# A hybrid RG-LRU, Conformer, cross-attention and conv-FFN layer: query weights and memory tokens turned as float32r, and the stages' order set anew

## Chip, cores and metric

The kernel runs on one core of a Trainium2 chip. The metric is device time in microseconds, the median of three runs. A core has a matrix engine (TensorE, PE in the profile; its loads of the stationary operand are PEld), a vector engine (VectorE, DVE), a scalar engine (ScalarE, ACT), GpSimd (POOL) and SyncE (SP), which here mostly issues DMAs. SBUF is the on-chip memory, PSUM the banks that TensorE writes.

## What is computed

One layer over x of 2048 tokens by 1024 channels and 256 memory tokens, all float32:

```python
h = rms_norm(x, mix_norm_g);  z = h @ w_in                    # 1024 -> 2048
lru_x, lru_gate, conf_a, conf_b = split(z, 4)                 # 512 each
y_lru = rg_lru(causal_dwconv(lru_x, 4 taps)) * gelu(lru_gate) # 8 heads of 64, scan over tokens
c = causal_dwconv(conf_a * sigmoid(conf_b), 31 taps)
c = silu(layer_norm(c))
x = x + concat([y_lru, c]) @ w_out

h = rms_norm(x, xa_norm_g);  m = rms_norm(mem, mem_norm_g)
q = h @ w_q;  k, v = split(m @ w_kv, 2)                       # 4 heads of 256
p = softmax(q @ k.T / 16)                                     # over 256 memory tokens
x = x + (p @ v) @ w_o

h = rms_norm(x, ffn_norm_g);  g, u = split(h @ w_up, 2)       # 3072 each
x = x + (gelu(causal_dwconv(g, 3 taps)) * u) @ w_down
out = rms_norm(x, final_norm_g)
```

## The kernel before

**Arithmetic.** Most matmuls run three times in float32r: each operand is split into a rounded part (ACT copies it into a float32r tile, names ending in h) and the rest (DVE subtracts, names ending in l), and hh, hl and lh are added up in PSUM (`mm3`). `split` and `split_scaled` do the splitting. A float32r tile has to be written by an instruction that writes that type; a float32 tile can't simply be read as one.

**Turning.** TensorE contracts over partitions, so tokens and weights are turned where their layout does not fit: `transpose` multiplies a 128 x 128 block by the identity (`ident`), as float32, four blocks into one PSUM bank. Turned are x (tiles `x`, `xn`), the softmax's output (`prob`), some gains, the memory tokens (`mem`, 16 blocks, in `memory_a`) and the query weights (`raw`, 64 blocks, in `operands` inside `memory_a`).

**Stages.** The tokens are worked in four blocks q of 512. For each block a mixer (`m[q]`: norm, projection by `w_in`, conv, LRU), a normalisation (`n[q]`) and attention (`a[q]`). Attention is folded: `memory_a` forms A = w_q k^T for each head (it needs the turned query weights and `kv`, the projection of the memory tokens by `w_kv`), and `memory_vo` forms v w_o; both are kept in DRAM. Blocks 2 and 3 are attended together (`attend_pair`) by a Strassen-like scheme of seven products, whose weights the task `fold` prepares. Then comes the feed-forward: `up` over two halves of 1024 tokens (`strassen_cols`, seven products for each pair of weight columns, operand sets B11, B21, T2, T1, T3, T4, B22, tiles `Xh` and `Xl`), and `Down` (tiles `hidh`, `hidl`, `wh`, `wl`).

`HalfX.make(key)` splits the four blocks of one operand set, each by an ACT copy and a DVE subtraction. `first_x` makes the first `EARLY` sets of the first half ahead of time; `up` makes the others when a product asks for them. For the second half, `up` makes each set in the last step of the first half, as soon as the set that it replaces has been used.

**Order.** The order of instructions is written out when the kernel is built, in two steps. First the stages are Python generators (`Task`); `drive` lets the first one in the list `TURNS` go on whose pause is over, counted in TensorE time. What a task yields is a pause or another task that it waits for; the constants (`MEM_WAIT`, `MIX_WAIT`, `ATT_PACE` and so on) are such pauses. Second, `Program` plans all operations on a model of the engines: it takes costs from `estimate`, a handover between engines of `HOP`, DMAs of `DMA_DELAY` plus bytes by `DMA_RATE`, ACT table switches (`ACT_SWITCH`, and `ACT_PATIENCE`, how near its due time an operation must be before a switch is made for it), gives each operation a due time, and picks on each engine the ready one that is due first. Operations made while `pr.first` is set come before all others. The best of `PASSES` plans is emitted. On the chip each engine then works through its list in that order and waits where an operand is late. DMAs are issued in the plan's order by SP, a few by ACT and POOL. Tiles come from 84 SBUF slots of 128 x 512 (`S`), a few larger ones, and 8 PSUM banks.

**The beginning.** `make_identity` builds `ident` on POOL, DVE sets a few constants, and `first_tokens` keeps TensorE busy with 16 turns of the identity while the first x and `w_in` pieces and the mixing gains (`in_mix_norm_g`, issued by ACT) arrive.

Nearly every instruction comes from `Program.emit`, so line 399 stands in almost every row of the profile, and rows are told apart by the tiles.

Of the kernel before, what the change touches and what calls it, by code (L numbers as in the profile page):

```python
# [12 lines left out]
F32R = mybir.dt.float32r  # L13
AF = mybir.ActivationFunctionType
# [3 lines left out]
P = 128  # L18
# [3 lines left out]
KQ = NK // 2  # L22
TT = 512
NQ = S // TT
# [3 lines left out]
M = 256  # L28
# [19 lines left out]
            AF.Gelu_apprx_tanh: (11,), AF.Silu: (18,)}  # L48


HOP = 0.3
HOP_SAME = 0.1
DMA_DELAY = 2.5
DMA_RATE = 300e3
ACT_SWITCH = 1.3
ACT_PATIENCE = 8.0
POOL_LAST = 6.0
ISSUE = dict(SP=0.1, ACT=0.3, Pool=1.0)
PASSES = 3
# [32 lines left out]
class Ref:  # L92
# [2 lines left out]

    def __getitem__(self, i):
        return Ref(self.buf, self.steps + (lambda ap: ap[i],), self.dummy[i])

    def f32(self):
        return Ref(self.buf, self.steps + (lambda ap: ap.bitcast(F32),), self.dummy)  # L100
# [32 lines left out]
class Program:  # L133
# [71 lines left out]
    def dma(self, out, in_, reads=(), writes=(), join=False, slack=30, by="SP"):  # L205
# [5 lines left out]
        nbytes = max(int(np.prod(r.dummy.shape)) for r in refs) * 4  # L211
        o.cost, o.delay = nbytes / DMA_RATE, DMA_DELAY
        o.calls.append(("dma_start", (), dict(out=out, in_=in_)))
# [25 lines left out]
    def deadlines(self, order):  # L239
# [10 lines left out]
        for o in reversed(self.ops):  # L250
            lat = o.cost + o.delay + HOP
            for s in o.succs:
# [7 lines left out]
    def schedule(self):  # L260
# [27 lines left out]
        def pick(e, t):  # L288
# [22 lines left out]
            if e == "ACT":  # L311
                o = h[0][2]
                if o.sets is not None and table[0] not in o.sets and o.due + lag[0] - t > ACT_PATIENCE:
                    other = [x for x in h if x[2].sets is None or table[0] in x[2].sets]
# [43 lines left out]
        while events:  # L358
# [11 lines left out]
            else:  # L370
                for s in o.succs:
                    satisfied(s, t + (HOP_SAME if s.eng == o.on else HOP))
                for b in o.bufs:
                    b.left -= 1
                    if b.left == 0:
                        free[b.tag].append(b.slot)
                        grant(b.tag, t + HOP)
        assert len(order) == len(self.ops)
# [44 lines left out]
def hybrid_layer(  # L423
# [7 lines left out]
    nc = tc.nc  # L431
# [9 lines left out]
    pr = Program(nc, place)  # L441

    def const(shape, name, dtype=F32):
        return Buf(None, shape, cpool.tile(list(shape), dtype, name=name), dtype, name)
# [10 lines left out]
    def transpose(o, in_, idn):  # L455
        pr.do("PE", "transpose", o, in_, idn)

    class together:
        def __enter__(self):
            pr.group = pr.op("PE")  # L460
# [10 lines left out]
    def rnd(name, shape=None):  # L471
        return pr.new("S", shape, F32R, name)
# [7 lines left out]
    def spawn(gen, before=None):  # L480
        t = Task(gen)
        tasks.insert(tasks.index(before) if before else len(tasks), t)
        return t
# [15 lines left out]
    ident_t = cpool.tile([P, P], F32, name="ident")  # L499
    make_identity(nc, ident_t)  # L500
    ident = Buf(None, (P, P), ident_t)
    ones_t = cpool.tile([P, P], F32, name="ones")
    nc.vector.memset(ones_t[:], 1.0 / DL)
    ones = Buf(None, (P, P), ones_t)
# [124 lines left out]
    def raw_cols(w, c0, kq):  # L629
        st = pr.new("W", (P, KQ, 2 * P), name="raw")  # L630
        pr.dma(st[:], w[kq * KQ * P : (kq + 1) * KQ * P, c0 : c0 + 2 * P].rearrange("(k p) f -> p k f", p=P))
        return st
# [119 lines left out]
    def turned(xs, take, wait=0):  # L752
        for k in range(NK):
            p = ps()
            with together():
                for tb in range(NTB):
                    transpose(p[:, tb * P : (tb + 1) * P], xs[tb][k // 4][:, (k % 4) * P : (k % 4 + 1) * P], ident[:])
            take(k, p)
            if k % 2:
                yield wait  # L760
# [191 lines left out]
    def memory_a():  # L952
        pr.first = True
        xs = []
        for mb in range(2):
            parts = []
            ssp = small(2)
            for half in range(2):
                t = tmp("mem")
                pr.dma(t[:], mem[0, mb * P : (mb + 1) * P, half * TT : (half + 1) * TT])  # L960
                ACT(junk[:], t[:], AF.Square, accum_out=ssp[:, half : half + 1])
                parts.append(t)
            r = small(1)
            V("tensor_tensor", r[:], ssp[:, 0:1], ssp[:, 1:2], op=ALU.add)
            ACT(r[:], r[:], AF.Sqrt, bias=eps[:], scale=1.0 / D)
            V("reciprocal", r[:], r[:])
            for t in parts:
                ACT(t[:], t[:], AF.Copy, scale=r[:, 0:1])
            xs.append(parts)
        for k2 in range(NK // 2):  # L970
            t = tmp("mt")
            p = ps()
            with together():
                for kk in range(2):
                    k = 2 * k2 + kk
                    for mb in range(2):
                        transpose(p[:, kk * M + mb * P : kk * M + (mb + 1) * P], xs[mb][k // 4][:, (k % 4) * P : (k % 4 + 1) * P], ident[:])
            for kk in range(2):
                sl = slice(kk * M, (kk + 1) * M)
                ACT(t[:, sl], p[:, sl], AF.Copy, scale=vec["v1024"][:, 2 * k2 + kk, G_MEM : G_MEM + 1])  # L980
            mt.append(t)
        pr.first = False
        yield MEM_WAIT
        def operands(h):
            kk = yield from kv(h * M)
            yield 0

            qt = []
            for kq in range(2):
                st = raw_cols(w_q[0], h * M, kq)  # L990
                for db in range(2):
                    p = ps()
                    with together():
                        for j in range(KQ):
                            transpose(p[:, j * P : (j + 1) * P], st[:, j, db * P : (db + 1) * P], ident[:])
                    hi, lo = pair("qt")
                    split(p[:], hi, lo)
                    qt.append((hi, lo))
            yield 1
            return kk, qt  # L1000

        nxt = yield from operands(0)
        for h in range(4):
            (kh, kl), qt = nxt
            if h < 3:
                nxt = yield from operands(h + 1)
            for k2 in range(NK // 2):
                p = ps()
                with together():
                    for kk in range(2):  # L1010
                        k = 2 * k2 + kk
                        for db in range(2):
                            hi, lo = qt[(k // KQ) * 2 + db]
                            cs = slice((k % KQ) * P, (k % KQ + 1) * P)
                            ks = slice(db * M, (db + 1) * M)
                            mm3(p[:, kk * M : (kk + 1) * M], hi[:, cs], lo[:, cs], kh[:, ks], kl[:, ks], db == 0, db == 1)
                t = pair("a")
                split(p[:], *t)
                for kk in range(2):
                    keep(A_rows, 2 * k2 + kk, h // 2, slice((h % 2) * M, (h % 2 + 1) * M), [b[:, kk * M : (kk + 1) * M] for b in t])  # L1020
                yield 0
            yield 0
# [56 lines left out]
    attended = [Task(None) for _ in range(NQ)]  # L1079
# [893 lines left out]
        yield V_LATE  # L1973
        vec["v3072"] = columns([ffn_conv_w[0], ffn_conv_b], DFF, "v3072")

    EARLY, VO_WAIT, V_LATE, Z_COPIED = 5, 2, 500, (0, 1)
    MIX_WAIT, MIX_TURN, LN_SUM, LN_SQ, GATES = (5, 7, 6, 0), 5, 6, 0, 3
    MIX_PACE, ATT_PACE = (1, 4, 3, 4), ((0, 3, 0), (0, 2, 2), (6, 3, 3), (5, 9, 0))
    PAUSE, WARM = 2, 16
    FED = ("B21", "T2", "T1", "T3")  # L1980
    MEM_WAIT, VO_LATE, ATT_TURN, FFN_TURN, X_PACE, T_PACE = 17, 10, 1, (3, 8, 7, 24), 3, 10

    FOLDED = (2, 3)
    PAIR_WAIT, PAIR_TURN, FOLD_PACE = (0, 0, 9, 17), 7, (6, 7, 35)
    EARLY_AT, KEPT_AT = 6, 5
    FOLD_AT = lambda: ([turned_x[0]], [mem_a, turned_x[1]], [mem_vo])
    F_out, F_a, F_vo = Folds(W_out, "t_out"), Folds(A_rows, "t_a"), Folds(VO_rows, "t_vo")

    NORMED = [lambda: ([m[0]], 108), lambda: ([attended[0]], 31), lambda: ([m[2]], 26), lambda: ([m[3], n[2]], 6)]
    ATTEND = [lambda: [n[0]], lambda: [n[1]]]  # L1990
    TURNS = lambda: [later, first, fold, m[0], mem_a, m[1], first_t, a[0], n[2], m[3], n[0], n[3], mem_vo, n[1], m[2], a[1], a[2], tail]
    X = [HalfX(h) for h in range(NH)]

    def first_x():
# [6 lines left out]
    def feed_forward():  # L2001
        yield first
        yield attended[NQ - 1]
        spawn(X[1].kept(attends[NQ - 1], 20), tail)
        spawn(prepare_down(), tail)
        yield from up(0, X[0], X[1].make)
        down = Down()

        def ahead(key):
            if key in FED:  # L2010
                down.feed(0, FED.index(key))

        yield from up(1, X[1], ahead)
        yield from down.run()

    mixers, normeds, attends = ([Task(None) for _ in range(NQ)] for _ in range(3))
    later, mem_a, mem_vo, first_t, first, tail = (Task(None) for _ in range(6))
    m, n, a = mixers, normeds, attends
# [7 lines left out]
    fold = Task(fold_weights())  # L2026
# [36 lines left out]
```

## Time and profile before

| What | Value |
|---|---|
| median of three runs | 2398.5 us (2398.17 to 2398.66) |
| span of the profiled execution | 2396.1 us, 2.4 us under the median |
| instructions | 33,483 |
| PE busy | 2382.6 us, 99% of the span, 10,948 matmuls |
| PEld busy (beside PE) | 1974.5 us, 82% |
| DVE busy | 2034.0 us, 85% |
| ACT busy | 1313.2 us, 55%, in it 75 table loads of 1.28 us |
| granted TensorE clock | 0.999 of full speed |
| DMA | 604.56 MB, mean 252 GB/s |

A row of a group reads: line, engine, operation, tiles written and read, shapes, number, then busy time, mean ns of one, and the idle time ahead of it with what ended it. A matmul's row names the moving operand first and then the stationary one: `ps<-ident,raw` is a turn of a piece of `raw`. Matmul records overlap, each lasts longer than the distance to the next, so a matmul's cost is read from the distance between starts. A row of the waits has the time in all, the number of times, and the longest. A row of stretches has the stretch, its length, busy time and count of each engine, the granted clock, the busy share of the DMA engines, and GB/s.

### The profile page before, as it was taken

How to read it: one execution, taken by the hardware profiler on the slowest of the kernel's cores; microseconds unless marked ns; L12 is line 12 of the kernel's file. 1: busy time of each engine (PE TensorE's matmuls, PEld its weight loads, DVE VectorE, ACT ScalarE, POOL GpSimd, SP SyncE). 2: the span in 40 equal slices, each digit the busy share in tenths (PEclk: the TensorE clock that was granted, in tenths of full speed). 3: DMA queues.
4: the chain of work that ended last, by engine and by line, in shares of the span. 5: the costliest groups of instructions: out<-in, count | busy, mean ns of one | idle time of the engine just before them, and what ended most of it. 6: DMA issues, size and time to landing. Idle time of an engine off the chain costs nothing.

```text
span 2396.1 us, 33483 instructions
## 1 busy us (share of the span) xinstructions
PE 2382.6 (99%) x10948; PEld 1974.5 (82%) x10948; DVE 2034.0 (85%) x3355; ACT 1313.2 (55%) x2374; POOL 11.2 (0%) x26
## 2 busy tenths in 40 slices
PE   9999999999999999999999999999999999999998
PEld 7898888888887888888888888888888888888887
DVE  7999994299899869879999887988988896676787
ACT  7772776357557678695555555554555541222333
POOL 1000000000000000000000000000000000000000
PEclk9999999999999999999999999999999999999999
DMA  9598789775878988787766544556565589887986
GB/s 351 197 296 309 234 300 305 254 255 176 296 261 271 318 277 280 268 289 265 252 234 208 194 172 158 175 177 211 190 216 199 186 303 324 283 280 254 312 303 258
DMA packets 363912, 604.56 MB, mean 252 GB/s; under 512 B 34809, under 2 KB 116985, under 8 KB 363738
## 3 DMA queue, kind: packets, MB, share of 16 engines
q1 hardware_dynamic: 362952, 601.81, 73.8%
q8 instruction: 86, 1.41, 0.2%
q14 instruction: 88, 0.72, 0.1%
q0 software_dynamic: 640, 0.36, 0.0%
q10 hardware_dynamic: 146, 0.27, 0.0%
HBM read 409.36 MB, written 192.94 MB: 251 GB/s over the span
## 4 chain that ended last, share of the span: by engine, by line
PE 94%; DVE 2%; ACT 2%; DMA 1%; issue 1%; SPq 0%; POOL 0%; DVEq 0%; POOLq 0%; ACTq 0%
PE ps L399 94%; DMA wl<-w_down 1%; DVE conv L399 1%; ACT L399 0%; DMA raw<-in_w_kv_dram 0%; ACT wh L399 0%; DVE wl L399 0%; ACT gate L399 0%; DVE x L399 0%; DVE s L399 0%; ACT yh L399 0%; DVE smalls L399 0%; DVE ptl L399 0%; ACT prob L399 0%; ACT conv L399 0%
## 5 line engine op out<-in xcount | busy, mean ns | idle before, releaser
L399 PE MATMUL ps<-Xh,wh 128*128 128x512 f32 x1344 | 523.3, 389 | 0.7 <-ACT u L399 0.7
L399 PE MATMUL ps<-Xh,wl 128*128 128x512 f32 x1344 | 523.2, 389 | 0.7 <-DVE wl L399 0.5
L399 PE MATMUL ps<-Xl,wh 128*128 128x512 f32 x1344 | 523.0, 389 | 0.0
L399 PE MATMUL ps<-wh,hidh 128*128 128x512 f32 x960 | 374.4, 390 | 0.0
L399 PE MATMUL ps<-wh,hidl 128*128 128x512 f32 x960 | 374.2, 390 | 0.1
L399 PE MATMUL ps<-wl,hidh 128*128 128x512 f32 x960 | 373.7, 389 | 0.0
L399 DVE SCALAR_TENSOR_TENSOR conv<-cb,v,conv 128x512 f32<-128x512 f32 x480 | 334.9, 741 | 1.8 <-ACT conv L399 0.9
L399 PEld LDWEIGHTS ps<-Xh,wl 128*128 128x128 f32 x1344 | 252.3, 188 | 54.0 <-DVE wl L399 1.5
L399 PEld LDWEIGHTS ps<-Xh,wh 128*128 128x128 f32 x1344 | 252.3, 188 | 53.1 <-ACT u L399 1.1
L399 PEld LDWEIGHTS ps<-Xl,wh 128*128 128x128 f32 x1344 | 252.3, 188 | 52.5
L399 ACT ACTIVATE hidh<-s 128x512 fp32r<-128x512 f32 x186 | 113.8, 631 | 271.6 <-DVE s L399 227.9
L399 PEld LDWEIGHTS ps<-wh,hidl 128*128 128x128 f32 x960 | 180.2, 188 | 39.5 <-DVE hidl L399 2.1
L399 PEld LDWEIGHTS ps<-wh,hidh 128*128 128x128 f32 x960 | 180.2, 188 | 37.8 <-ACT hidh L399 0.4
L399 PEld LDWEIGHTS ps<-wl,hidh 128*128 128x128 f32 x960 | 180.3, 188 | 37.2 <-DMA wl<-w_down 0.4
L399 PE MATMUL ps<-xh,wh 128*128 128x512 f32 x512 | 204.0, 398 | 0.1
L399 PE MATMUL ps<-xl,wh 128*128 128x512 f32 x512 | 199.6, 390 | 0.3 <-DVE xl L399 0.3
L399 PE MATMUL ps<-xh,wl 128*128 128x512 f32 x512 | 199.6, 390 | 0.0
L399 ACT ACTIVATE wh<-s 128x512 fp32r<-128x512 f32 x192 | 119.6, 629 | 117.6 <-DVE s L399 79.1
L399 ACT ACTIVATE wh<-raw 128x512 fp32r<-128x512 f32 (+2 forms) x214 | 127.4, 613 | 53.1 <-PE ps L399 21.6
L399 ACT ACTIVATE u<-ps 128x512 f32<-128x512 f32 x144 | 85.7, 595 | 126.0 <-PE ps L399 125.2
L399 DVE TENSOR_TENSOR acc<-acc,ps 128x512 f32<-128x512 f32 (+1 forms) x157 | 102.7, 678 | 59.5 <-PE ps L399 56.4
L399 DVE TENSOR_TENSOR wl<-raw,wh 128x512 fp32r<-128x512 f32 (+2 forms) x214 | 140.2, 668 | 12.0 <-ACT wh L399 10.7
(256 smaller groups left out, 4014.2 us busy)
## 6 DMA issues: line engine op xcount, KB each, us to landing
raw<-in_w_up_dram SPq DMA_DIRECT2D x96, 512.0 KB, 4.5
wh<-w_down SPq DMA_DIRECT2D x156, 256.0 KB, 4.9
wl<-w_down SPq DMA_DIRECT2D x156, 256.0 KB, 5.0
w_down<-wh SPq DMA_DIRECT2D x144, 256.0 KB, 3.1
w_down<-wl SPq DMA_DIRECT2D x144, 256.0 KB, 3.5
h<-hid SPq DMA_DIRECT2D x120, 256.0 KB, 4.7
wh<-w_in SPq DMA_DIRECT2D x96, 256.0 KB, 4.2
wl<-w_in SPq DMA_DIRECT2D x96, 256.0 KB, 4.7
```

The source lines that it names most:

```text
L399: getattr(e, name)(*[resolve(a) for a in args], **{k: resolve(a) for k, a in kw.items()})
```

## The change

Three parts.

1. A second identity, `ident_r`, in float32r, is written once by ACT at the very beginning. `turn_block` turns a float32r block with it, into the PSUM bank read as float32r.
2. The memory tokens, after ACT has scaled them, are copied by DMA from their four SBUF tiles into four float32r tiles `xr` (256 KB each), and turned from there. Each half piece of the query weights is copied from `raw` into two such tiles, 16 transfers of 256 KB in all, and turned from there. A DMA moves the bits unchanged.
3. The constants of the order are other ones: the planner's `HOP`, `DMA_RATE` and `ACT_PATIENCE`, most pauses, `EARLY` (five operand sets to one), and the list `TURNS`.

```diff
-HOP = 0.3
+HOP = 0.15
-DMA_RATE = 300e3
+DMA_RATE = 350e3
-ACT_PATIENCE = 8.0
+ACT_PATIENCE = 4.0
...
+    def f32r(self):
+        return Ref(self.buf, self.steps + (lambda ap: ap.bitcast(F32R),), self.dummy)
...
+    def turn_block(o, src, cs):
+        if src.dtype == F32R:
+            transpose(o.f32r(), src[:, cs], ident_r[:])
+        else:
+            transpose(o, src[:, cs], ident[:])
+
+    def carried(t):
+
+        b = rnd("xr")
+        pr.dma(b[:].f32(), t[:])
+        return b
...
     ident = Buf(None, (P, P), ident_t)
+    ident_r = const((P, P), "identr", F32R)
+    nc.scalar.activation(ident_r.real[:], ident_t[:], AF.Copy)
...
-            xs.append(parts)
+            xs.append([carried(t) for t in parts])
...
-                        transpose(p[:, kk * M + mb * P : kk * M + (mb + 1) * P], xs[mb][k // 4][:, (k % 4) * P : (k % 4 + 1) * P], ident[:])
+                        turn_block(p[:, kk * M + mb * P : kk * M + (mb + 1) * P], xs[mb][k // 4], slice((k % 4) * P, (k % 4 + 1) * P))
...
                 st = raw_cols(w_q[0], h * M, kq)
+                rs = [rnd("xr") for _ in range(2)]
+                for db in range(2):
+                    pr.dma(rs[db][:].split2(KQ).f32(), st[:, :, db * P : (db + 1) * P])
                 for db in range(2):
                     p = ps()
                     with together():
                         for j in range(KQ):
-                            transpose(p[:, j * P : (j + 1) * P], st[:, j, db * P : (db + 1) * P], ident[:])
+                            turn_block(p[:, j * P : (j + 1) * P], rs[db], slice(j * P, (j + 1) * P))
...
-    EARLY, VO_WAIT, V_LATE, Z_COPIED = 5, 2, 500, (0, 1)
-    MIX_WAIT, MIX_TURN, LN_SUM, LN_SQ, GATES = (5, 7, 6, 0), 5, 6, 0, 3
-    MIX_PACE, ATT_PACE = (1, 4, 3, 4), ((0, 3, 0), (0, 2, 2), (6, 3, 3), (5, 9, 0))
-    PAUSE, WARM = 2, 16
+    EARLY, VO_WAIT, V_LATE, Z_COPIED = 1, 2, 500, (0, 1)
+    MIX_WAIT, MIX_TURN, LN_SUM, LN_SQ, GATES = (13, 7, 1, 0), 4, 11, 0, 3
+    MIX_PACE, ATT_PACE = (1, 4, 3, 4), ((0, 3, 1), (2, 0, 2), (0, 0, 0), (0, 0, 0))
+    PAUSE, WARM = 1, 16
...
-    MEM_WAIT, VO_LATE, ATT_TURN, FFN_TURN, X_PACE, T_PACE = 17, 10, 1, (3, 8, 7, 24), 3, 10
+    MEM_WAIT, VO_LATE, ATT_TURN, FFN_TURN, X_PACE, T_PACE = 0, 10, 1, (4, 18, 0, 0), 17, 18
...
-    PAIR_WAIT, PAIR_TURN, FOLD_PACE = (0, 0, 9, 17), 7, (6, 7, 35)
-    EARLY_AT, KEPT_AT = 6, 5
+    PAIR_WAIT, PAIR_TURN, FOLD_PACE = (3, 2, 7, 28), 2, (11, 7, 35)
+    EARLY_AT, KEPT_AT = 4, 0
...
-    NORMED = [lambda: ([m[0]], 108), lambda: ([attended[0]], 31), lambda: ([m[2]], 26), lambda: ([m[3], n[2]], 6)]
+    NORMED = [lambda: ([m[0]], 107), lambda: ([attended[0]], 29), lambda: ([m[2]], 28), lambda: ([m[3], n[2]], 9)]
...
-    TURNS = lambda: [later, first, fold, m[0], mem_a, m[1], first_t, a[0], n[2], m[3], n[0], n[3], mem_vo, n[1], m[2], a[1], a[2], tail]
+    TURNS = lambda: [n[2], fold, later, n[3], m[0], mem_a, m[1], m[3], n[0], first, first_t, n[1], a[0], mem_vo, m[2], a[1], a[2], tail]
...
-        spawn(X[1].kept(attends[NQ - 1], 20), tail)
+        spawn(X[1].kept(attends[NQ - 1], 24), tail)
```

More of the change, by code (lines that the diff above doesn't have):

```diff
@@ L756, in turned @@
                 for tb in range(NTB):
-                    transpose(p[:, tb * P : (tb + 1) * P], xs[tb][k // 4][:, (k % 4) * P : (k % 4 + 1) * P], ident[:])
+                    turn_block(p[:, tb * P : (tb + 1) * P], xs[tb][k // 4], slice((k % 4) * P, (k % 4 + 1) * P))
             take(k, p)
```

## Prediction

> **What bounds the kernel now.** First the page: the span, the busy time of each engine, and the chain that ended last.
>
> ```profile
> span 2396.1 us, 33483 instructions
> PE 2382.6 (99%) x10948; PEld 1974.5 (82%) x10948; DVE 2034.0 (85%) x3355; ACT 1313.2 (55%) x2374; POOL 11.2 (0%) x26
> PE 94%; DVE 2%; ACT 2%; DMA 1%; issue 1%; SPq 0%; POOL 0%; DVEq 0%; POOLq 0%; ACTq 0%
> ```
>
> TensorE is busy in 99% of the span and carries 94% of the chain. So a change can save time in two ways only: fewer TensorE nanoseconds, or shorter TensorE waits. Next, how much wait there is. The list of who waited for whom, for TensorE alone, is short (four of its eight rows stand here, the others are 0.5 us and less); below it stand the piece of the chain at which the last matmul ends, and four stretches of the feed-forward part.
>
> ```profile
> PE ps L399 <- POOL ident masks.py:199: 2.4, 1, 2.4
> PE ps L399 <- DMA raw<-in_w_kv_dram: 1.5, 1, 1.5
> PE ps L399 <- ACT u L399: 0.7, 1, 0.7
> PE ps L399 <- DVE wl L399: 0.5, 1, 0.5
> ...
> 2368.58 20.93 PE ps L399 x91
> ...
> core 0: us, PE busy (x) PEld busy (x) DVE busy (x) ACT busy (x) POOL busy (x), PEclk, DMA share, GB/s
> 1050.00:1100.00 50.00, 50.00 (x239) 41.91 (x238) 43.50 (x71) 35.53 (x58) 0.00 (x0) 1.00 0.86 297
> 1200.00:1250.00 50.00, 50.00 (x222) 41.43 (x221) 45.98 (x77) 25.77 (x41) 0.00 (x0) 1.00 0.67 234
> 1450.00:1500.00 50.00, 49.31 (x217) 40.23 (x216) 39.15 (x62) 27.32 (x47) 0.00 (x0) 1.00 0.52 173
> 1500.00:1550.00 50.00, 49.31 (x218) 40.48 (x217) 49.41 (x79) 30.85 (x47) 0.00 (x0) 1.00 0.48 160
> ```
>
> The reader is to see three things. Idle time is 2396.1 - 2382.6 = 13.5 us; 2.4 of it is the start (the identity), and 6.6 the end (the last matmul ends at 2368.58 + 20.93 = 2389.5), so 4.5 us lie inside. A stretch without a wait holds 222 matmuls in 50 us: 0.225 us from one 512-column float32r matmul to the next. And where TensorE shows 0.69 us idle twice (1450 to 1550), 9 matmuls are missing, 2.0 us of work for 1.4 us of idle: records overlap, so real waits are some 1.5 times the idle shown. All waits inside are thus worth about 6.7 us, 0.28% of the span. That is the most a new order alone could win; nothing bounds what it could lose.
>
> The span is 2.4 us below the median of the runs, 2398.5. I make the sum on the span and carry the 2.4 us over.
>
> **The turning, 80 transposes.** Sixteen turn memory tokens, 64 turn query weights (4 heads, 2 halves, 2 column blocks, 4 each). Rows: what they take, the time of each engine's own load, and groups of small matmuls in order of time, each with the row behind it, so that the spacing can be read.
>
> ```profile
> L399 PE MATMUL ps<-ident,raw 128*128 128x128 f32 x64 | 7.6, 273 | 0.0
> ...
> L399 PEld LDWEIGHTS ps<-kvh,qth 128*128 128x128 f32 x64 | 12.3, 192 | 0.0
> L399 PEld LDWEIGHTS ps<-ident,raw 128*128 128x128 f32 x64 | 7.2, 141 | 0.4
> ...
> 113.30 1.91 PE L399 MATMUL ps<-ident,raw 128*128 128x128 f32 x16
> 115.05 2.32 PE L399 MATMUL ps<-mt,raw 128*128 128x256 f32 x10
> ...
> 123.94 0.28 PE L399 MATMUL ps<-kvh,qtl 128*128 128x256 f32 x1
> 124.06 0.28 PE L399 MATMUL ps<-kvh,qth 128*128 128x256 f32 x1
> ...
> 283.75 0.95 PE L399 MATMUL ps<-ones,sum 128*128 128x1 f32 x8
> 284.56 3.70 PE L399 MATMUL ps<-mt,raw 128*128 128x256 f32 x16
> ...
> 523.67 1.15 PE L399 MATMUL ps<-ident,raw 4*128 4x4 f32 x16
> 524.75 0.50 PE L399 MATMUL ps<-wh,yh 128*128 128x512 f32 x1
> ```
>
> The 272 ns is latency; the cost is the spacing, (115.05 - 113.30)/16 = 109 ns. No float32r matmul of 128 columns is in the trace. Two float32r sizes are: 225 ns at 512 columns, 120 ns at 256. The line through them, 0.41 ns a column and 15 ns beside, gives 67 ns at 128. The other limit is the load of the stationary operand: 16 turns of 4 columns, each with 128 weight columns, come every (524.75 - 523.67)/16 = 67 ns, so a load in turning mode fits into 67 ns. I take 65 ns: 80 x (109 - 65) = 3.5 us less TensorE time, all on the path, since TensorE has no slack. Ends: 62 ns (a little under both rows), 3.8 us; and no better row than the full 225 ns on the bad side, 80 x 116 = 9.3 us lost, which I hold for unlikely, as that row moves four times the columns.
>
> Against it: the load for a float32r matmul lasts 192 ns, for a turn 141, and eight full-width matmuls that move one column (283.75) still need (284.56 - 283.75)/8 = 101 ns each. If a float32r turn loads like these, it comes every 101 to 109 ns and the gain is 0 to 0.6 us. The Trainium skill, TensorE: Matmul & The Clock Gate, section LDWEIGHTS, says that a load takes its columns divided by 1.2, in ns, whatever the rows; an estimate of 107 ns for 128, and by it the turning would gain 0.2 us. The 101 ns agrees, the 67 ns of the small turns does not, and they are turns. Its section Back-to-back issue gap gives about 81 ns for load and matmul pairs of 128 columns, by which the gain would be 2.2 us; no run here shows such a pair.
>
> **The transfers, 20 of 256 KB.** Rows: DMA issues of the first 60 us and of 88 to 170 with their median time to landing, two stretches (DMA share next to last), and the last work on the memory tokens with the first weight loads of the key projection, which multiplies them.
>
> ```profile
> x<-in_x_dram SPq DMA_DIRECT2D x8, 256.0 KB, 5.3
> mem<-in_mem_dram SPq DMA_DIRECT2D x4, 256.0 KB, 5.8
> ...
> w_in<-wh SPq DMA_DIRECT2D x2, 256.0 KB, 2.2
> wh<-w_in SPq DMA_DIRECT2D x2, 256.0 KB, 7.5
> ...
> 0.00:50.00 50.00, 47.31 (x239) 39.33 (x240) 37.13 (x96) 35.46 (x73) 11.18 (x26) 1.00 0.99 352
> 100.00:150.00 50.00, 48.50 (x297) 43.46 (x296) 49.80 (x80) 41.74 (x80) 0.00 (x0) 1.00 0.68 223
> ...
> L399 PE MATMUL ps<-ident,mem x16: 270/272/273, 49.3 to 50.9; 128*128 128x128 f32 x16
> L399 ACT ACTIVATE mem<-mem,smalls x4: 708/711/712, 44.8 to 47.9; 128x512 f32<-128x512 f32 x4
> ...
> L399 PEld LDWEIGHTS ps<-mt,raw x256: 186/190/193, 93.5 to 287.7; 128*128 128x128 f32 x128
> ```
>
> No transfer inside SBUF is in the trace; by these rows one takes 2.2 to 7.5 us. Each issue also takes its turn on SP, and the four of the tokens are queued there behind the ACT scaling that ends at 47.9 + 0.7 = 48.6, so loads behind them on SP wait with them. The tokens now turn at 49.3; they would be ready at 51 to 56. The first matmul that needs them is at 93.5 now, so cover is long, but the planner puts these turns first of all and reckons 2.5 us plus 0.75; where DMAs are 99% busy a transfer takes up to 3 us more than that, and TensorE would stand for it. 0 to 3 us; I take 0.5. The 16 of the weights have the projections and attention work beside them (DMAs 68% busy); 0, at worst 3 us, twice the one DMA wait of 1.5 us that this phase shows now.
>
> **The new identity.** One ACT copy of 128 x 128 stands ahead of everything on ACT, so also ahead of the DMA issue for the mixing gains.
>
> ```profile
> 0.74 0.53 ACTq L399 DMA_DIRECT2D raw<-in_mix_norm_g_dram  x1
> 3.06 0.29 ACT L399 ACTIVATE full<-ones 128x128 fp32r<-128x128 f32 x1
> 2.03 0.32 POOL masks.py:199 TENSOR_SCALAR_AFFINE_SELECT ident<-ident 128x128 f32<-128x128 f32 x1
> 6.86 0.75 PE L399 MATMUL ps<-ident,raw 1*128 1x1 f32 x8
> ```
>
> It waits for the identity (2.35), so the issue slides from 0.74 to about 2.5; with the 5.3 us of the x loads the gains land at 7.8 at worst, and they are turned at 6.86. 0 to 0.9 us; I take 0, as it is one row of 4 KB.
>
> **The order.** `MEM_WAIT` 17 to 0 sets the memory projections 17 us of TensorE time earlier; I take the 1.5 us wait for `w_kv` as gone (at worst it stays or doubles). `EARLY` 5 to 1 leaves four more operand sets of the feed-forward to be split when its products run.
>
> ```profile
> L399 DVE TENSOR_TENSOR Xl<-tx,Xh x32: 659/684/694, 1024.5 to 1501.9; 128x512 fp32r<-128x512 f32 x32
> L399 DVE TENSOR_TENSOR Xl<-xn,Xh x24: 680/684/693, 1013.0 to 1517.4; 128x512 fp32r<-128x512 f32 x24
> ```
>
> That is 16 x 0.684 = 10.9 us of VectorE moved to the first products after 1043, where it is busy 43.5 of 50 us. The second half's sets are made in the same late way today, at 1457 to 1517, and that costs the 2.0 us read above. So 0 to 2.0; I take 1.0, as the planner may pull some ahead. If VectorE could pull nothing ahead, 10.9 less the 6.5 us of slack leaves 4.4, and without any slack 10.9. In the new `TURNS` the tasks ahead of `later` wait for others, so POOL's queue, which `later` fills, begins as it did. The other new values (pauses, `HOP`, `DMA_RATE`, `ACT_PATIENCE`) only place the same instructions elsewhere, and ACT, 55% busy, has room for a few more table loads: 0, from -5.2 (every other wait inside goes) to the 10.9 above.
>
> **Sum:** -3.5 + 0.5 + 0 - 1.5 + 1.0 = -3.5; span 2392.6, time 2395.0.
>
> **Rivals and chances.** A change under 0.2% (4.8 us) can't be told from none.
> - The forecast, 0.42: turns at 65 ns, waits in sum much as now. 2395.0, by itself 2392 to 2398; a third of it (0.14) falls under 2393.7.
> - The turns gain nothing, 0.20: they are bound by the load. -0.6 + 0.5 - 1.5 + 1.0 = -0.6, 2397.9. For it the 192 ns loads and the 101 ns row, against it the 67 ns row.
> - The new order also takes most waits away, 0.22: -3.8 - 5 = 2389.7, at the least -3.8 - 6.7 = 2388. For it: every wait inside is a single one, not a shortage. Against: each reshuffle makes its own.
> - Slower, 0.13: VectorE becomes the bound at the start of the feed-forward, with 10.9 us of splits and no cover: -3.5 + 0.5 - 1.5 + 10.9 = +6.4, 2404.9. For it VectorE's 43.5 and 46.0 of 50 us there; against, the 2.0 us that the same work costs at 1500. It decides from 8.3 us of new waits on.
> - The float32r turn is slower than now, 0.03: at most 2398.5 + 9.3, less the rest, 2407.
>
> Faster 0.14 + 0.22 = 0.36, same 0.28 + 0.20 = 0.48, slower 0.16. Range 2387.5 to 2405, which leaves out the worst of the slow cases.
>
> **What would show it.** Turns in float32r with starts 60 to 70 ns apart (or 101 and more); TensorE's list without `w_kv`; a wait for `Xl` or `wl` near the first feed-forward product, whose worth is the number of matmuls short of 222 in 50 us; TensorE standing for a transfer just ahead of the token turns. The forecast is wrong if the waits inside, by that count, leave the 3 to 10 us band.

## The result, and the profile after

The changed kernel takes 2410.34 us (median of five runs, 2407.9 to 2413.24); the kernel before took 2398.5 (five runs, 2396.98 to 2398.66). The ratio is 1.0051, 95% interval 1.0039 to 1.0063: slower by some 12 us, where 3.5 us less was forecast. Its profiled execution has a span of 2408.3 us, against 2396.1. First the page's busy times, and the chain's shares by engine.

```profile
span 2408.3 us, 33476 instructions
PE 2386.4 (99%) x10948; PEld 1974.8 (82%) x10948; DVE 2038.1 (85%) x3355; ACT 1300.9 (54%) x2368; POOL 11.2 (0%) x26
PE 80%; DVE 11%; DMA 6%; ACT 1%; issue 1%; SPq 0%; POOL 0%; DVEq 0%; ACTq 0%; POOLq 0%
```

TensorE's idle time went from 13.5 to 2408.3 - 2386.4 = 21.9 us; its busy time rose by 3.8 us although the turns became shorter. VectorE and DMAs now hold 17% of the chain, where they held 3%. The waits of TensorE, first six rows:

```profile
PE ps L402 <- DVE smalls L402: 3.9, 1, 3.9
PE ps L402 <- POOL ident masks.py:199: 2.4, 1, 2.4
PE ps L402 <- DVE vol L402: 2.0, 1, 2.0
PE ps L402 <- DVE gb L402: 1.8, 3, 0.7
PE ps L402 <- DVE ptl L402: 1.8, 2, 1.0
PE ps L402 <- DVE up L402: 1.0, 4, 0.3
```

The wait for `w_kv` is gone, as forecast; the longest is a new one, said to be for VectorE's `smalls`. Its place in the timeline of TensorE tells more (start, length, instruction, idle ahead of it); the first two rows are the first float32r turns and what follows them.

```profile
62.93 1.49 PE L402 MATMUL ps<-identr,xr 128*128 128x128 f32 x16
64.25 0.46 PE L402 MATMUL ps<-xh,wh 128*128 128x512 f32 x1
...
147.62 2.75 PE L402 MATMUL ps<-mt,raw 128*128 128x256 f32 x12
154.28 1.53 PE L402 MATMUL ps<-identr,xr 128*128 128x128 f32 x8 [3.90 <-DVE smalls L402]
```

TensorE stood at the turns of a `xr` tile, which are the last head's query weights. The tile comes by a transfer, so SP's timeline is the next view, with the transfers' times to landing below.

```profile
139.11 0.45 SPq L402 DMA_DIRECT2D raw<-in_w_q_dram  x1
139.61 1.31 SPq L402 DMA_DIRECT2D x<-in_x_dram  x2
141.02 0.41 SPq L402 DMA_DIRECT2D raw<-in_w_q_dram  x1
141.52 5.68 SPq L402 DMA_DIRECT2D x<-in_x_dram  x6
147.56 1.62 SPq L402 DMA_DIRECT2D A<-ah  x2
149.50 1.29 SPq L402 DMA_DIRECT2D xr<-raw  x2
...
L402 SPq DMA_DIRECT2D xr<-raw x16: 594/606/997, 90.6 to 155.0; - x16
DMA to landing us min/median/max: 2.5/3.6/4.6
```

The weights were asked for at 139.11 and 141.02, together with eight pieces of x. SP could issue the hop to `xr` at 149.50, when they were there; it landed 4.6 us later, the longest of the five landings that the trace has for these sixteen transfers, and the turns start at 154.28, 4.8 us after its issue. `smalls` ended at that moment by chance: the wait is for the transfer. Four stretches around it (granted clock and DMA share are the columns before the last):

```profile
core 0: us, PE busy (x) PEld busy (x) DVE busy (x) ACT busy (x) POOL busy (x), PEclk, DMA share, GB/s
140.00:150.00 10.00, 10.00 (x61) 9.19 (x60) 6.95 (x12) 3.45 (x8) 0.00 (x0) 1.00 1.04 367
150.00:154.28 4.28, 0.38 (x2) 0.03 (x1) 4.28 (x9) 4.12 (x13) 0.00 (x0) 0.96 1.03 342
154.28:160.81 6.53, 6.44 (x32) 6.29 (x33) 6.20 (x12) 4.70 (x9) 0.00 (x0) 0.51 0.84 280
160.81:170.00 9.19, 9.19 (x81) 9.19 (x80) 8.24 (x14) 8.93 (x16) 0.00 (x0) 1.00 0.98 331
```

The DMA engines were taken up fully, 103 to 104%. After the wait the clock was granted by half for 6.53 us: 6.53 x (1 - 0.51) = 3.2 us more lost, which no list of waits shows, since TensorE counts as busy. 3.9 + 3.2 = 7.1 us at this one place. The 2.0 us wait for `vol` at 265 us and many small waits add to it; the gone `w_kv` wait and the shorter turns take some 3.6 us off.

### The profile page after: what moved, and what is told of

The parts are those of the page before. It is cut to its first block, busy times and chain, and to the rows that moved or that the text cites. A ratio compares the mean times of both kernels' runs of the same rounds, so it can differ in the third digit from the quotient of the medians.

```text
span 2408.3 us, 33476 instructions
## 1 busy us (share of the span) xinstructions
PE 2386.4 (99%) x10948; PEld 1974.8 (82%) x10948; DVE 2038.1 (85%) x3355; ACT 1300.9 (54%) x2368; POOL 11.2 (0%) x26
## 4 chain that ended last, share of the span: by engine, by line
PE 80%; DVE 11%; DMA 6%; ACT 1%; issue 1%; SPq 0%; POOL 0%; DVEq 0%; ACTq 0%; POOLq 0%
PE ps L402 80%; DVE conv L402 3%; DVE wl L402 2%; DVE cv L402 1%; DVE s L402 1%; DMA wh<-w_in 0%; ACT wh L402 0%; DVE xc L402 0%; DMA w_down<-wl 0%; DMA w_in<-wl 0%; DVE up L402 0%; DMA wh<-VO 0%; DMA wl<-w_down 0%; DVE xl L402 0%; DMA x<-in_x_dram 0%
## 5 line engine op out<-in xcount | busy, mean ns | idle before, releaser
L402 DVE TENSOR_TENSOR wl<-raw,wh 128x512 fp32r<-128x512 f32 (+2 forms) x214 | 142.3, 674 | 12.0 <-ACT wh L402 11.5
L402 DVE TENSOR_TENSOR wl<-s,wh 128x512 fp32r<-128x512 f32 x192 | 131.0, 689 | 19.1 <-ACT wh L402 13.5
```

What stands on the lines that cost most here:

```text
L402: getattr(e, name)(*[resolve(a) for a in args], **{k: resolve(a) for k, a in kw.items()})
```

## The experiments

A stretch without waits repeats exactly, so the distances between matmul starts, compared between two kernels, give the time lost in each region, the half clock included. The table has the excess over each form's median distance in the kernel before, worked out from all 10,948 starts of a profile, for the stretches from 0 to 1045 us and for the feed-forward's two parts, `up` and `Down`. The whole difference before and after is in it: 30.7 - 18.4 = 12.3 us. Only 6.8 of the 18.4 us stand at matmuls with idle time ahead of them (16.8 in after); most of the rest lies where a matmul of one form follows another, and is no wait. The last column has how long the half clock was granted ahead of the kernel's end.

| Kernel | us | ratio [95%] | 0-60 | 60-340 | 340-1045 | up | down | half clock, us |
|---|---|---|---|---|---|---|---|---|
| before | 2398.5 | 1 | 2.4 | 4.8 | 6.6 | 2.3 | 2.3 | 0 |
| after | 2410.34 | 1.0051 | 2.4 | 11.5 | 8.1 | 5.2 | 3.4 | 6.8 |
| e1: transfers, old constants | 2409.20 | 1.0047 [1.0034, 1.0059] | 2.1 | 16.2 | 5.9 | 2.3 | 2.3 | 13.7 |
| e2: new constants, no transfers | 2412.24 | 1.0059 [1.0046, 1.0072] | 3.9 | 11.2 | 8.8 | 6.9 | 2.8 | 3.4 |
| e3: after, float32 turns | 2409.19 | 1.0056 [1.0043, 1.0070] | 2.5 | 11.8 | 9.1 | 3.9 | 1.7 | 3.4 |
| e4: after, wait filled | 2411.77 | 1.0056 [1.0043, 1.0069] | 3.5 | 6.1 | 10.0 | 5.2 | 1.2 | 3.4 |
| e5: after, last head direct | 2407.05 | 1.0037 [1.0024, 1.0049] | 3.5 | 11.1 | 7.5 | 3.4 | 2.9 | 3.4 |
| p3: before, planner's three values | 2417.53 | 1.0075 [1.0063, 1.0088] | 2.7 | 14.1 | 10.3 | 8.8 | 2.1 | 3.4 |
| r3: before, DMA_RATE 350e3 | 2410.15 | 1.0057 [1.0043, 1.0071] | 3.8 | 12.9 | 9.0 | 5.2 | 3.3 | 6.8 |
| s1: before, new stage constants | 2401.20 | 1.0015 [1.0007, 1.0024] | 1.9 | 3.4 | 12.4 | 1.3 | 1.3 | 0 |

(The 36 turns that fill e4's wait count as work, so its 60-340 leaves out the 3.9 us of the wait. The turns are counted at 109 ns throughout, so the 60-340 of after, e1, e4 and e5 is low by the some 2 us that shorter turns save; e3's is not. The ratios are to runs of the kernel before beside each one. A row is of one profiled execution, and those of one kernel lie up to 6.5 us apart (p3, 2411.74 to 2418.24): r3's and e4's are 3.7 and 1.8 us above their medians. Cells that differ by 2 or 3 us show nothing by themselves.)

### The two halves of the change

**The transfers alone** (e1): all constants as before.

```diff
-HOP = 0.15              +HOP = 0.3
-DMA_RATE = 350e3        +DMA_RATE = 300e3
-ACT_PATIENCE = 4.0      +ACT_PATIENCE = 8.0
...                      (and the pauses and TURNS of before)
```

> The changed kernel with all constants of the order as they were; the transfers and the float32r turns stay. Theory 1 (the transfer in front of the turns costs: one wait of 4.1 us at 150 us plus 6.5 us at half clock behind it, 3.2 us, of the 12 us lost): the turns save 80 x (109 - 86 ns) = 1.8 us, and whether TensorE stands for a transfer depends on how busy the DMAs are where the old order puts the turns; 2397 if nowhere, up to 2405 with one such wait. Theory 2 (the new constants alone cost the 12 us): 2396.7.

2409.2 us, ratio 1.0047 [1.0034, 1.0059]. The longest waits of TensorE between 60 and 340 us:

```profile
PE ps L402 <- ACT qth L402: 2.8, 1, 2.8
PE ps L402 <- DMA xr<-raw: 2.7, 3, 1.5
PE ps L402 <- ACT xh L402: 2.7, 1, 2.7
```

The first two lie on the path from `xr` to the turned query weights (`qth`); the third, ahead of 77.8 us, is a wait of the mixer that the new plan brought. 6.8 us of half clock follow each of the two places. So the transfers, with the plan that comes of them, cost 12 us on the constants that were good without them, above the 2405 expected at most; nearly half of the loss lies at the mixer's place, which by its row is no wait for a transfer. At the query weights the DMAs were not what was slow here: the last head's weights had landed by 151.7 us, but SP's list had stores of A ahead of the hop, which was issued at 159.76 and landed in 2.5 to 2.9 us.

**The constants alone** (e2): the kernel before with every new constant.

> The kernel before with all new constants of the order; turned straight from raw as float32, no transfers. Theory 1: the wait at 150 us and the half clock go, the turns cost 1.8 us more, the other 5 us of new waits stay: 2405, give or take 3 as the plan is made anew. Theory 2: 2412.

2412.24 us, ratio 1.0059 [1.0046, 1.0072]: 15 us, and no transfer is in it. The two halves, 12 and 15, do not add up to 27; together they cost 12. e1 loses its time between 60 and 340 us alone; e2 loses 6.4 us there (11.2 against 4.8) and the other 9 elsewhere, 4.6 of them in `up`.

**The turns' type alone** (e3): the same plan, `xr` as float32.

```diff
-        b = rnd("xr")
-        pr.dma(b[:].f32(), t[:])
+        b = tmp("xr")
+        pr.dma(b[:], t[:])
...
-                rs = [rnd("xr") for _ in range(2)]
+                rs = [tmp("xr") for _ in range(2)]
```

> The changed kernel with the carried tiles declared float32 and turned with the float32 identity; transfers, plan and order of all instructions are those of the changed kernel. Only the turns' spacing differs, 109 for 86 ns: both theories say 1.8 us more than the changed kernel, 2412; less where turns lie beside a wait. If the float32r turn were what costs, this would be faster than 2410.

2409.19 us, ratio 1.0056 [1.0043, 1.0070], not told apart from after's. What the float32r turns save (below) is not seen in the time: the slower turns arrive later, and the wait is that much shorter. TensorE's waits between 60 and 340 us, and two stretches:

```profile
PE ps L402 <- DVE vol L402: 2.3, 1, 2.3
PE ps L402 <- DVE smalls L402: 1.6, 1, 1.6
...
262.00:267.00 5.00, 2.70 (x12) 1.95 (x11) 5.00 (x9) 2.58 (x6) 0.00 (x0) 0.99 0.74 239
267.00:271.00 4.00, 4.00 (x12) 2.89 (x13) 4.00 (x7) 0.77 (x3) 0.00 (x0) 0.59 1.01 344
```

The wait at 150 fell from 3.9 to 1.6 us, and its half clock is gone; instead the wait for `vol` grew from 2.0 to 2.3 us and now half clock follows it.

### The wait at 150 us

**Without the last head's transfers** (e5): its four transfers left out, its turns from `raw`, the plan unchanged.

```diff
+                    if h == 3:
+                        pr.ops[-1].calls.clear()
...
+                        if h == 3:
+                            pr.group.calls = [("transpose", (p[:, j * P : (j + 1) * P], st[:, j, db * P : (db + 1) * P], ident[:]), {}) for j in range(KQ)]
```

> The changed kernel, its order of instructions kept, but for the last of the four heads the four transfers are left out and the 16 blocks are turned straight from raw as float32. Theory 1: the query weights have landed at 149.5, TensorE comes at 150.4, so the wait of 4.1 us and the half clock behind it (3.2 us) go: 2403 to 2404. Theory 2: the wait only passes to the next late operand (the copies of k, behind squares on ACT that wait for x), 2408 or more.

2407.05 us, ratio 1.0037 [1.0024, 1.0049], some 3 us under after, with intervals that overlap. Two stretches at the old place of the wait and at `vol`, then TensorE's waits between 60 and 340 us:

```profile
150.00:160.00 10.00, 9.71 (x76) 9.09 (x75) 10.00 (x19) 9.03 (x22) 0.00 (x0) 1.00 0.79 270
...
267.00:271.00 4.00, 4.00 (x12) 2.88 (x10) 4.00 (x8) 1.04 (x3) 0.00 (x0) 0.57 0.98 335
...
PE ps L402 <- DVE vol L402: 2.3, 1, 2.3
PE ps L402 <- DVE xl L402: 1.5, 1, 1.5
```

That the wait at 150 was for the transfer is shown: it is gone, though `smalls` is still computed. But its 7.1 us did not come back as time: TensorE, no longer held there, ran into `xl` and `vol`, and into a half clock of its own (4.00 x 0.43 = 1.7 us).

**With the wait filled** (e4): 36 more turns of the identity, ahead of the turns that wait.

```diff
+                        if (h, kq, db) == (3, 0, 0):
+                            pr.group.calls += [("transpose", (p[:, :P], ident[:], ident[:]), {})] * 36
```

> The changed kernel, order kept, with 36 more turns of the identity (36 x 0.109 = 3.9 us) just ahead of the turns of the last head that wait for the transfer at 150 us: TensorE works through the wait, so the wait stays and the clock has no reason to halve. If the half clock of 154 to 161 us is the idle time's doing, it goes and with it 3.2 us: 2407. If it comes from elsewhere: 2410.

2411.77 us, ratio 1.0056 [1.0043, 1.0069]: nothing won. Stretches:

```profile
150.00:154.28 4.28, 4.28 (x34) 4.05 (x34) 4.28 (x7) 4.12 (x13) 0.00 (x0) 1.00 1.10 375
154.28:160.81 6.53, 6.53 (x62) 6.53 (x61) 6.53 (x14) 6.06 (x13) 0.00 (x0) 1.00 0.85 279
...
262.00:270.00 8.00, 5.68 (x25) 4.39 (x24) 8.00 (x13) 4.13 (x9) 0.00 (x0) 1.00 0.50 164
270.00:275.00 5.00, 5.00 (x18) 3.24 (x17) 5.00 (x9) 1.02 (x4) 0.00 (x0) 0.66 0.97 316
```

The half clock came from the idle time, for it is gone when the idle time is filled with idle work. Yet the matmuls that now ran at full speed met late operands afterwards: again `vol`, until 269 us, with a half clock there.

Where both gains went is seen when the same matmul is looked up in the profiles of after, e5 and e4, which keep one order. At 144 us of after, e5 and e4 are both 1.1 us late; at 164 they are 4.8 and 1.9 us early; at 277 they are 0.7 and 3.5 us late. So both gains are as good as gone before 280 us, and e5's shorter time comes from later stages. VectorE tells why. Its wait for ACT's copy of `w_o`, its busy time in the 65 us behind it, and the late `vol`, all in after:

```profile
200.74 1.29 DVE L402 TENSOR_TENSOR wl<-raw,wh 128x512 fp32r<-128x512 f32 x2 [2.86 <-ACT wh L402]
...
200.00:265.00 65.00, 65.00 (x292) 54.46 (x290) 64.16 (x101) 19.46 (x42) 0.00 (x0) 1.00 0.69 248
...
266.58 0.71 DVE L402 TENSOR_TENSOR vol<-ps,voh 128x512 fp32r<-128x512 f32 x1
```

From the first `vol` of this stretch (201.95) to the one that TensorE waits for (266.58) VectorE has no pause. This takes 64.6 us in after, e3, e4 and e5 alike, whenever TensorE comes; so what TensorE wins ahead of it turns into a longer wait behind it. In the kernel before VectorE is as full (65.00 of 65 us), but its first `vol` is at 195.07, without a wait ahead of it, and TensorE does not stand for the last.

### Which constants

**The planner's three values alone** (p3), **then each alone** (r2, r3, r4), on the kernel before:

```diff
-HOP = 0.3               +HOP = 0.15              (p3, r2)
-DMA_RATE = 300e3        +DMA_RATE = 350e3        (p3, r3)
-ACT_PATIENCE = 8.0      +ACT_PATIENCE = 4.0      (p3, r4)
```

> The kernel before with the planner's HOP, DMA_RATE and ACT_PATIENCE of the change and nothing else of it. Theory 3: 2404 to 2412, like any other plan. If those three values are the culprit: 2408 or more, above the other two new plans. If the stage constants are: 2397 to 2400.

> The kernel before with HOP 0.15 for 0.3 alone. If the handover time is what makes the planner's list too tight: 2410 to 2418, with VectorE at 266 to 269 us of the 280 from 60 to 340. If not: 2397 to 2401, as with HOP 0.29.

> The kernel before with DMA_RATE 350e3 for 300e3 alone. If the planner's belief in faster transfers is the culprit, ACT and VectorE stand behind loads that are listed too early: 2410 to 2418. If not: 2397 to 2401.

> The kernel before with ACT_PATIENCE 4 for 8 alone: ACT holds to its table up to 4 us ahead of the due time, not 8. If operations on ACT then come too late for VectorE: 2410 to 2418. If not: 2397 to 2401.

p3 2417.53 (1.0075 [1.0063, 1.0088]), r2 2404.54 (1.0031 [1.0020, 1.0043]), r3 2410.15 (1.0057 [1.0043, 1.0071]), r4 2399.99 (1.0014 [1.0005, 1.0023]). So over their own runs of before the three cost 20 us, the rate alone 13, `HOP` 7.5, `ACT_PATIENCE` 3. ACT's waits between 60 and 340 us, of the kernel r3:

```profile
ACT wh L399 <- DMA raw<-in_w_o_dram: 10.0, 3, 5.8
```

and of after:

```profile
ACT wh L402 <- DMA raw<-in_w_o_dram: 8.9, 3, 5.0
...
ACT junk L402 <- DMA x<-in_x_dram: 5.9, 2, 5.7
```

The kernel before has no wait for `w_o` there. Planned with faster DMAs, ACT takes up the splitting of `w_o` (near 195 us) before the loads have landed, and everything in its list behind stands too, VectorE with it (2.86 us in after, above). e2, e3, e4, e5 and p3 stand for `w_o` in the same way, for 8.1, 12.8, 13.6, 11.1 and 9.9 us. The kernels planned at 300e3 have at most 1.9 us of it (s3, below, for `voh`). And a TensorE wait of 2.0 to 2.7 us for `vol` near 265 us, or a half clock starting there, is in all of after, e2, e3, e4, e5, p3 and r3, but in none of before, e1, s1, r1 and s3. r2 has neither, and its 7.5 us, between what its two cases expected, lie outside 60 to 340 us; what `HOP` does there is open.

**The stage constants alone** (s1): the pauses, `EARLY` and `TURNS` of after, the planner's values of before, no transfers.

> The kernel before with the new stage constants alone (TURNS, pauses, EARLY and the rest); planner's values and turns as before. If the stage constants have a price of their own: 2405 or more, with VectorE at 266 to 270 us busy of the 280 from 60 to 340. If the loss of the change is the planner's rate and the transfers: 2397 to 2402.

2401.2 us, ratio 1.0015 [1.0007, 1.0024]: 3 us, with none of it in 60 to 340; in the profiled execution it lies at 340 to 1045 (12.4 against 6.6), while the feed-forward wins 2.

**`EARLY` alone, by one set** (p4), and **a value moved by almost nothing** (p2):

```diff
-    EARLY, VO_WAIT, V_LATE, Z_COPIED = 5, 2, 500, (0, 1)     (p4)
+    EARLY, VO_WAIT, V_LATE, Z_COPIED = 4, 2, 500, (0, 1)
...
-HOP = 0.3                                                    (p2)
+HOP = 0.29
```

> The kernel before with EARLY 4 for 5. Theory 3: 2404 to 2412. Theory 2: 2397 to 2400, as one operand set is 4 x 0.68 us of VectorE work that moves by a few us. The step of the prediction on EARLY (0 to 2 us for four sets) says 2398 to 2399.

> The kernel before with one constant of the planner a little off, HOP 0.29 for 0.3: a new plan of the same work, with no transfer and no new stage order. Theory 3 (the order before is one that happens to have few waits; any new plan of so full a TensorE brings some 10 us of them): 2404 to 2412. Theory 2 (the new constants are bad by their values): 2397 to 2400.

p4 2400.07 (1.0013 [1.0004, 1.0022]), p2 2398.86 (1.0005 [0.9996, 1.0014]). One set less costs 2.6 us, in the profile in `up`; a plan that merely differs costs nothing clear of noise, which refutes that any new plan of this kernel is worse.

### Mending the plan around the transfers

**After with the planner's values of before** (r1), **with the old rate alone** (s3), and **e1 with the hop planned for** (s2):

```diff
-HOP = 0.15              +HOP = 0.3               (r1)
-DMA_RATE = 350e3        +DMA_RATE = 300e3        (r1, s3)
-ACT_PATIENCE = 4.0      +ACT_PATIENCE = 8.0      (r1)
...
+        pr.ops[-1].delay = 6.0                   (s2, after each of the two pr.dma of the hop)
```

> The changed kernel with the planner's three values (HOP, DMA_RATE, ACT_PATIENCE) as they were; stage constants, transfers and float32r turns stay. Theory 4 (the planner's values are the larger loss: with them operations are listed before their operands are there, VectorE stands for ACT in the stretch of 60 to 340 us where it has no slack, 269 of 280 us busy for 276.5 before): 2398 to 2404. Theory 2 (the stage constants cost): 2408 or more.

> The changed kernel with DMA_RATE 300e3 for 350e3 alone. If the rate makes ACT stand for the w_o loads (8.9 us in the changed kernel, 0 in all kernels at 300e3), that wait goes, and VectorE's late output at 265 us with it: 2 to 6 us less, 2404 to 2408, the transfer's wait left. If the wait moves: 2410.

> The transfers and float32r turns on the old constants, with the planner told that such a transfer lands 6.0 us after its bytes, not 2.5 (the slow ones took 4.7 us in all). If TensorE's waits of 2.7 us for the transfers and the half clock behind come from the planner's belief alone, they go: 2396 to 2399, the turns' 1.8 us with them. If the transfers themselves crowd SP and the DMAs: 2405 or more.

r1 2414.6 (1.0072 [1.0059, 1.0085]), s3 2418.54 (1.0090 [1.0076, 1.0103]), s2 2435.34 (1.0157 [1.0143, 1.0171]). None mends it, and s3 came out above both of its cases. In r1 and s3 the wait for `w_o` is gone (0.2 and 1.9 us are left) and `xr<-raw` stands in its place (4.2 and 3.8 us) with 13.7 and 10.2 us of half clock: with the transfers and the new stage constants in, the higher rate is the better one. On the old stage constants it was not tried with the transfers. In s2, TensorE's waits between 150 and 200 us:

```profile
PE ps L402 <- DMA xr<-raw: 17.6, 1, 17.6
PE ps L402 <- DVE qtl L402: 7.4, 1, 7.4
```

The hop, planned to be slow, was put behind stores and loads in SP's list and was issued at 175.58 only, after `w_q` at 159.0 and 161.7: allowing for a late transfer made it later.

**A rate on the other side** (t3): the kernel before, planned with slower DMAs.

```diff
-DMA_RATE = 300e3
+DMA_RATE = 250e3
```

> The kernel before with DMA_RATE 250e3 for 300e3. If what the rate of 350e3 costs (13 us) is the belief that transfers come sooner than they do, a slower rate should cost nothing: 2396 to 2400. If the planner's values only fit each other: 2404 or more.

2517.43 us, ratio 1.0500 [1.0485, 1.0514]. Its waits are all over the kernel:

```profile
PE ps L399 <- ACT hidh L399: 15.0, 11, 3.1
PE ps L399 <- ACT xh L399: 11.9, 3, 6.0
PE ps L399 <- DVE xl L399: 9.6, 9, 2.2
```

So 300e3 has a fall on both sides, 13 us above and 120 us below.

### Is VectorE the second bound?

**Twelve VectorE operations fewer** in after (t1) and in before (t2): taps of the 31-tap convolution left out, 8 us of VectorE.

```diff
+                    if row is not None and t > 27:
+                        pr.ops[-1].calls.clear()
```

> The changed kernel, order kept, with 3 of the 31 taps of the Conformer convolution left out for the first 512 tokens: 12 VectorE operations of 0.66 us, 8 us, gone from the stretch of 60 to 340 us. Theory 5 (in that stretch VectorE, 276 of 280 us busy before, is a second bound, so time that it loses there becomes TensorE waits): the waits behind VectorE there (2.0 us at 265 and what follows) go, the transfer's wait stays: 2404 to 2407. If VectorE has slack there: 2410.

> The same 12 operations left out of the kernel before. There TensorE waits 1.5 us for a weight load in that stretch and for VectorE next to nothing, so both theories say 2396 to 2398.5.

t1 2408.35 (1.0045 [1.0033, 1.0058]), t2 2397.37 (1.0000 [0.9991, 1.0009]). TensorE's waits of t1 between 60 and 340 us:

```profile
PE ps L402 <- DVE smalls L402: 3.6, 1, 3.6
PE ps L402 <- DVE vol L402: 0.4, 1, 0.4
```

The wait for `vol` is VectorE's lateness: 8 us less work takes it from 2.0 to 0.4, as the 64.6 us between the two `vol` become 63.0. The wait at 150 does not care, as befits a transfer. But the whole kernel wins 1 to 2 us, with intervals that overlap, and before wins nothing; VectorE's lateness at this place is a part of the loss, not the whole.

## Why the prediction was wrong, point by point

**The 16 weight transfers: 0, at worst 3.** This step failed. It priced the hop by how busy the DMAs were on average (68%) and took attention work as cover. What counts is the one moment where the last head's weights come: they were asked for only ten us earlier, the DMAs were at 103 to 104%, and a hop that cannot start before its source has landed took 4.6 us. 3.9 us of waiting is just above the bound; the 3.2 us of half clock behind it were in no term at all. e1 prices the transfers, with the plan that comes of them, at 12 us on the old constants.

**"The other new values only place the same instructions elsewhere: 0."** This failed too, and is the larger error. They cost 15 us with the transfers left out (e2), most of it through `DMA_RATE` (13 by itself). The range given, -5.2 to 10.9, was taken from other mechanisms, and so were both cases that made the kernel slower: what came had no place among them. The view for it was there: VectorE's busy time in the stretch that lost, before and after:

```profile
60.00:340.00 280.00, 278.35 (x1393) 234.88 (x1392) 275.54 (x433) 181.56 (x327) 0.00 (x0) 1.00 0.78 262
```

```profile
60.00:340.00 280.00, 273.77 (x1372) 230.10 (x1371) 269.07 (x423) 179.76 (x333) 0.00 (x0) 0.99 0.81 273
```

Before, TensorE was busy for 99.4% of these 280 us and VectorE for 98.4%. A list of waits that is almost empty does not mean room: two engines were full at once, and ACT and SP had to feed both in order, so that a hold of VectorE at 200 us came back as a wait of TensorE at 265. The start of the feed-forward, where the prediction looked for VectorE as the bound, was not the place, though in the two profiles `up` has 2.9 us of the loss in all (5.2 against 2.3).

**The turns: -3.5 us.** Sixteen turns take (64.25 - 62.93)/16 = 82 ns, not 65; 80 x (109 - 82) = 2.1 us. The term was mis-sized, and neither the forecast's 62 to 67 ns nor the rival's 101 to 109 holds. The Trainium skill, TensorE: Matmul & The Clock Gate, section Back-to-back issue gap, gives about 81 ns for a load and matmul pair of 128 columns; the trace's 82 ns agree. On equal plans even these 2.1 us did not show (e3).

**The steps that held.** The tokens' transfers: in after, no wait ahead of the turns at 62.93. The identity at the start: the first wait is 2.4 us in both. The `w_kv` wait is gone. `EARLY`: two stretches of after at the first products and at the second half's sets,

```profile
1050.00:1100.00 50.00, 50.00 (x238) 41.88 (x237) 40.72 (x66) 39.12 (x68) 0.00 (x0) 1.00 0.64 230
1450.00:1500.00 50.00, 50.00 (x222) 41.40 (x221) 40.91 (x66) 28.59 (x47) 0.00 (x0) 1.00 0.65 209
```

show 238 matmuls where there were 239, and no idle time: VectorE had the splits ready, and the slower rival by 10.9 us of splits did not come. (p4's 2.6 us for one set say that the price depends on the plan, so the term of 1.0 is not settled.) The estimate of the waits inside, 6.7 us, agrees with the 6.8 us of excess at matmuls behind idle time. "The new order takes most waits away" did not come either. The sum missed because its two zeros stood for the two things that could hurt.

**What stays open.** The parts do not add: transfers 12, planner's values 20, stage constants 3, all together 12. Where VectorE sets the time at 265 us, losses ahead of it cover each other, which is one reason why the sum is less than the parts; why it is 12 is not shown. 5.5 of after's 12.3 us lie outside 60 to 340 us, in waits of at most 1.0 us each that no run took away by themselves. That the hold of VectorE at 200 us makes `vol` late is read from the traces above and from which kernels have both; no run took away the wait for `w_o` and left the rest as it was. No kernel tried that computes the whole layer beats the one before; p2, with the same time, is the nearest.

## What to carry to other kernels

Where a list of waits is nearly empty, ask which other engine is also full in that stretch, and give a changed order or a changed model value a range for loss as wide as the kernel's slack is small; a zero needs its cover named at the tightest moment, not on average. An extra hop between a load and its first use is paid where the load is the last one: here by a landing of 4.6 us beside full DMAs, in e1 by 8 us in SP's list. When a wait has been taken away, look at what is late next before counting its microseconds: here two cures of a 7 us loss had lost all they won 120 us later, at an engine that has no pause.

## What the runs showed of the hardware

- A TensorE wait of a few microseconds can cost twice. After 3.9 us the clock was halved for some 6.8 us (e1, after two places: 13.7 in all); in e3, 2.3 us were followed by 3.4 us of it, while 2.0 us at the same place in after (below) and 2.4 us at 147 us in p3 were not. The lengths come in steps of 3.4 us. The Trainium skill, TensorE: Matmul & The Clock Gate, section What's actually happening, has the clock fall after an idle window of about 3.4 us; the steps agree, but here half clock followed a wait of 2.3 us, and in e2 one of 1.5 us at 177 us, so a single wait need not fill a window. No limit for it comes out of these runs.

```profile
267.00:271.00 4.00, 3.66 (x18) 2.66 (x18) 4.00 (x8) 1.88 (x5) 0.00 (x0) 1.00 0.96 363
```

- Idle turns of the identity (e4) kept the clock full through the same 4 us.
- A transfer of 256 KB inside SBUF took 2.5 to 4.6 us from issue to landing in the five of the sixteen weight transfers of after whose landing the trace has. The longest stood beside full DMAs (share 1.03), but full DMAs alone do not make it long: in e1 one took 2.9 us at a share of 1.01.
- The engine that a wait is put down to can be one that merely ended at that moment (`smalls`); the timeline of the tile's own transfer decides.
